# Second feed-forward block of a decoder trunk: the down products of its first two chunks in seven block products

## The chip, the cores and the metric

The kernel runs on one core of a Trainium2 chip. Five engines work beside each other: TensorE (PE, with its weight loads as PEld), VectorE (DVE), ScalarE (ACT), GpSimd (POOL) and SyncE (SP); SP and POOL also issue transfers, each from its own queue. Every engine works through its instructions in order, and waits where an instruction needs the result of another engine or a buffer that is still in use. Matrix products are accumulated in PSUM, in banks of 128 partitions x 512 numbers; everything else lies in SBUF. The metric is the device time of one execution in microseconds.

## The reference, cut to what matters

One step of a trunk with 512 new prompt tokens and 8 sample tokens (520 in all), width 1024, hidden width 2816, all in float32:

```python
h = h + 0.5 * _swiglu(_rms_norm(h, ffn1_norm), w_gate1, w_up1, w_down1)     # FFN1
m, p, c, s = _hybrid_mixer(_rms_norm(h, mix_norm), st_pool, st_conv, st_ssm, ...)
h = h + m
h = h + 0.5 * _swiglu(_rms_norm(h, ffn2_norm), w_gate2, w_up2, w_down2)     # FFN2
return _rms_norm(h, final_norm), new_pool, new_conv, new_ssm

def _swiglu(x, wg, wu, wd):
    return (jax.nn.silu(x @ wg) * (x @ wu)) @ wd

# a sample's new recurrent state (8 samples, 16 heads of 64 x 128):
#   new = exp(dt * A) * old + (dt * x) outer B
```

The new state of each sample is an output that nothing else in the step reads.

## The kernel before, in words

**Numbers in two parts.** Each operand of a large product is cut into a high part and a low part. ScalarE casts the high part, and VectorE subtracts it from the original to get the low part (`split`, L126 and L128; `part`, L228 and L229). Elsewhere a low part is made by a transfer: ScalarE writes minus the high part, and a transfer on POOL's queue adds the original out of memory onto it (`part_by_dma`, L225; L380 and L381 in `load`). `mm3` (L137 to L142) makes a product out of three matmuls of 128 x 128 by 128 x 260: high by high (L138), high by low (L141), low by high (L142). The 520 tokens are two halves of 260.

**Gate and up in seven block products.** The hidden width is 22 tiles of 128. For a tile f the gate and up weights, two halves of the width and two halves of the tokens form products of 2 x 2 blocks, which are made in seven block products for eight. Each is 4 x 3 = 12 matmuls, so a tile is 84. The weights come into a raw pair of buffers (`raw_pair`, two loads of 512 KB). VectorE makes sums of them: s1 of 1024 columns (L409) and s2 in two halves of 512 (L410, L411). These sums are cut into parts shi and slo: "c" from s1, used by products 7 and 5, and "d" from s2, used by 6 and 3. "a" is the first raw half itself, used by products 1 and 2. The last quarter "b" of the raw pair (`quarter`) serves product 4, which is issued in the next tile, right after that tile's product 1. The products accumulate in a bank A and in a double bank BE. ScalarE copies some of them out (L472), VectorE adds them, and `gates`, `silu` and `close` turn them into the gated hidden value.

**FFN1 (`stream`, L527).** Its 22 tiles f go in chunks of 8, 8 and 6. After each of the first two chunks come four Down tiles, `Down(c, d)`: the down product of this chunk for two of the eight output tiles, again in seven block products of 12 matmuls. For this the hidden values are kept in pairs (gq), and `keep_g` (L323) makes seven sums out of each pair of gate values in two parts (gs). The third chunk is done plainly (`down`). In FFN1 the first matmul group of every product is pinned: the products go out in program order.

**FFN2 (`rest`, `step`, `down`, `down_by_half`).** The gate and up products are the same. The down products of its first two chunks are plain: 8 output tiles x 2 halves of the tokens x 8 hidden tiles x 3 = 384 matmuls for a chunk. The third chunk goes by halves of the tokens, so that the final norm can start early. Only two products are pinned; for the rest the order is a planner's, which fills TensorE's queue with whatever is ready by its own estimate. So plain down products and hidden tiles are mixed at the border between them.

**The new states (`new_states`, L1133 on).** There are 16 steps. In each, POOL's queue loads a row `br` (64 KB) and the old state `hs` (256 KB); ScalarE makes `so`, four instructions of 128 x 128 (L1152); VectorE makes hs = hs * sdec + so, four instructions (L1154); POOL's queue stores the result (L1156). `STATES` says how many of these steps go ahead of each output tile of the three plain down products of FFN2. Their buffers, three `br`, three `hs` and two `so`, lie in a pool of their own, st2.

**Homes of weight parts.** Three pairs of whi and wlo (1024 columns each) rotate for the "a" parts and plain down weights (`weight_homes`, L116). `queued` puts an instruction behind a named one on its engine.

Of the kernel before, what the change touches and what calls it, by code (L numbers as in the profile page):

```python
# [17 lines left out]
P = 128  # L18
# [18 lines left out]
NG = 9  # L37
ON_ACT = 4
STATES = ((0, 1, 1, 1, 2, 1, 1, 1), (0, 1, 1, 1, 1, 0, 0, 0), (1, 0, 1, 0, 1, 0, 1, 0))
# [24 lines left out]
def tile_trunk_step(ctx: ExitStack, tc: tile.TileContext, ins: dict, outs: dict):  # L64
# [49 lines left out]
    homes = []  # L114

    def weight_homes(n, name, hp, nb, tags):  # L116
        if hp is wp:
            hp, nb, tags = homes.pop(0) if len(homes) > 1 else homes[0]
        return tuple(hp.tile([P, 1024], F32R, tag=t, bufs=nb, name=f"{t}_{name}")[:, :n] for t in tags)
# [53 lines left out]
    def squares(nx, wx, d, name, home=None):  # L173
        if d == 0:
            nc.scalar.activation(out=nx[2], in_=h[:, d], func=AF.Square)
            return
        sq = home
        if home is None:
            sq = wx.tile([P, 2, HB], F32, tag="tg", bufs=2, name=f"sq_{name}_{d}").rearrange("p b t -> p (b t)")
# [68 lines left out]
    class Ffn:  # L248
# [4 lines left out]
        def __init__(self, nx, i, wx, gp, direct):  # L253
            self.nx, self.i, self.wx, self.gp, self.direct = nx, i, wx, gp, direct
            self.states = None
            self.whole = (2,)
            self.folded = CHUNKS[0] + CHUNKS[1] if i == 1 else 0
            self.held = {} if self.folded else {CHUNKS[0] + 1: None, CHUNKS[0] + CHUNKS[1] + 1: None}
            self.dram, self.gs, self.pairs, self.few, self.later = {}, {}, {}, [], []
# [47 lines left out]
        def gate_home(self, f):  # L307
            if not self.folded:
                return self.wx.tile([P, 2, HB], F32, tag="tg", bufs=2, name=f"tg{self.i}_{f}")
# [13 lines left out]
        def keep_g(self, f, tg):  # L323
            if f >= self.folded:
                if self.folded:
                    if not self.few:
                        self.few = self.cells(f"g{self.i}_{f}")
                    g = self.few.pop().rearrange("p (a b) t -> p a b t", a=2)
                else:
                    g = self.gp.tile([P, 2, 2, HB], F32R, tag="g", bufs=NG, name=f"g{self.i}_{f}")  # L330
                self.g[f] = g
# [16 lines left out]
        def plain_out(self, f):  # L348
# [6 lines left out]
            if f and self.folded:  # L355
# [5 lines left out]
        def load(self, f, first, then, by_dma):  # L361
# [11 lines left out]
            with queued(*first):  # L373
                if self.folded and (f, 0) not in LOW_ON_DVE:
# [14 lines left out]
        def sums(self, f, n, src, raw, d1, by_dma):  # L389
            i, wx = self.i, self.wx  # L390
            s1 = wx.tile([P, 2, 512], F32, tag="sw", bufs=2, name=f"s1_{n}")
            s2 = wx.tile([P, 2, 512], F32, tag="sw", bufs=2, name=f"s2_{n}")
# [4 lines left out]
            else:  # L397
# [3 lines left out]
                s1, s2 = (t.rearrange("p q (j c) -> p q j c", j=4) for t in (s1, s2))  # L401
# [6 lines left out]
            else:  # L408
                nc.vector.tensor_tensor(out=s1, in0=diag, in1=up0, op=ALU.add)  # L409
            nc.vector.tensor_tensor(out=s2[:, 0], in0=s1[:, 1], in1=halves[0][:, 0], op=ALU.add)  # L410
            nc.vector.tensor_tensor(out=s2[:, 1], in0=s2[:, 0], in1=halves[0][:, 1], op=ALU.add)  # L411
            s1, s2 = (t.rearrange("p q c -> p (q c)" if len(t.shape) == 3 else "p q j c -> p (q j c)") for t in (s1, s2))
# [14 lines left out]
        def quarter(self, f, src):  # L427
            n = f"{self.i}_{f}b"
            if self.folded:
                hi, lo = (self.wx.tile([P, 512], F32R, tag=t, name=f"{t}_{n}") for t in ("qhi", "qlo"))  # L430
                h, l = hi, lo
                if len(src.shape) == 3:
                    h, l = (t.rearrange("p (j c) -> p j c", j=4) for t in (hi, lo))
                if isinstance(f, int) and f <= 6 and (f, 1) not in LOW_ON_DVE:
                    home = self.dram[f][1]
                    home = home[:, 512:] if isinstance(f, int) else home.rearrange("p (j q c) -> p q j c", q=2, c=P)[:, 1]
                    part_by_dma(h, l, src, home)
                else:
                    part(h, l, src)
                self.w[f][4] = (hi, lo), range(4)  # L440
                return
            self.w[f][4] = split(src, 512, n, wp, 3, ("whi", "wlo")), range(4)

        def product(self, f, p):
# [7 lines left out]
            if p != 1 and 4 not in self.w[f]:  # L452
                self.quarter(f, self.held[f])
            slot, dst, opens = {1: (0, 0, True), 2: (1, 1, True), 5: (3, 2, True), 6: (5, 0, False),
                                3: (2, 2, False), 7: (4, 0, False), 4: (6, 0, False)}[p]
            opens = opens and (p != 2 or self.i == 2 or f in self.whole)
# [11 lines left out]
            if p == 1 and self.i == 1 and f not in self.whole:  # L468
# [9 lines left out]
        def sum(self, f, home=None):  # L478
            be, a = self.BE[f][:, :, :HB], self.ac[f][0]
            if self.i == 2:  # L480
                nc.vector.tensor_tensor(out=home, in0=be, in1=a, op=ALU.add)
                return home
# [4 lines left out]
        def gates(self, f):  # L487
# [12 lines left out]
            nc.vector.tensor_tensor(out=tg, in0=self.sum(f, tg), in1=self.nx[3].rearrange("p (b t) -> p b t", b=2), op=ALU.mult)  # L500
            if self.i == 2:
                self.silu(f)

        def silu(self, f):
            tg = self.tg[f]
            with queued(*(() if self.i == 2 else (self.copied,))):
# [3 lines left out]
        def close(self, f):  # L510
# [8 lines left out]
            if self.i == 1:  # L519
                self.silu(f)  # L520
# [7 lines left out]
        def stream(self, before, last_chunk):  # L528
# [6 lines left out]
            for t in tiles:  # L535
                self.product(t, 1)
# [7 lines left out]
                if t == 5:  # L544
# [6 lines left out]
            before()  # L551
            self.down(len(CHUNKS) - 1, self.folded, KF, last_chunk)

        def rest(self, before, last_chunk):
            lo = 0
            for c, n in enumerate(CHUNKS):
                hi = lo + n
                last = hi == KF
                for f in range(self.direct if c == 0 else lo + 1, hi if last else hi + 1):
                    self.step(f)  # L560
                if last:
                    self.product(KF - 1, 4)
                    with tc.high_priority():
                        self.close(KF - 1)
                    wd = before()
                else:
                    self.product(hi + 1, 1)
                    self.product(hi, 4)
                    self.close(hi)
                if last and wd is not None:  # L570
                    self.down_by_half(c, lo, last_chunk, wd)
                else:
                    self.down(c, lo, hi, last_chunk if last else None)
                lo = hi

        def step(self, f):
            if f not in self.A:
                self.product(f, 1)
            if f - 1 not in self.g and f > self.direct:
                self.product(f - 1, 4)  # L580
                self.close(f - 1)
            for p in (2, 5, 6, 3, 7) if f in (2, KF - 1) else (5, 6, 3, 7, 2):
# [845 lines left out]
```

## Time and profile before

| | us |
|---|---|
| median of three runs | 975.1 (974.69 to 975.95) |
| the profiled execution | 974.41 |
| its span in the trace | 972.6 |
| TensorE busy | 960.5 (99%) |
| VectorE busy | 825.9 (85%) |
| ScalarE busy | 591.1 (61%) |
| POOL busy | 112.7 (12%) |

The granted clock of TensorE is 0.996 over the span. FFN1 takes about the first third, the mixer the second, FFN2 the last third from about 630 us on. Times of rows are in microseconds unless marked ns. A group of rows is one line of the kernel, an engine, an operation and the tiles that it writes and reads; its mean is the length of one instruction, and neighbours on TensorE overlap. "Idle before" is the time in which the engine stood still ahead of such an instruction, and behind the arrow stands what ended it. The chain is followed back from the last instruction, at each step to what released it.

### The profile page before, as it was taken

The numbers are of one execution on the slowest core, as the hardware profiler recorded it, in microseconds if no ns is written. First come the engines' busy times: TensorE is split into PE (matmuls) and PEld (weight loads), VectorE is DVE, ScalarE is ACT, GpSimd is POOL, SyncE is SP. The second block draws the span as 40 slices with busy tenths as digits, with TensorE's granted clock in tenths as the row PEclk, the third lists the DMA queues.
The fourth block names the chain that finished last, engine by engine and source line by source line (L and its number), as shares of the span: only waits on it lengthen the run. The fifth ranks groups of instructions, "written<-read, shape, count | busy, mean of one in ns | idle before, by whom it ended". The sixth has DMA issues, their size and how long they took to land.

```text
span 972.6 us, 19624 instructions
## 1 busy us (share of the span) xinstructions
PE 960.5 (99%) x7772; PEld 942.4 (97%) x7772; DVE 825.9 (85%) x1374; ACT 591.1 (61%) x1098; POOL 112.7 (12%) x192
## 2 busy tenths in 40 slices
PE   9999999999999999999999999999999999999995
PEld 8999999999999999999999999999999999999995
DVE  6999889899897698789888997999957999667886
ACT  7777666676566455485668655666643666515573
POOL 0111101000010001146331000100013000110010
PEclk9999999999999999999999999999999999999998
DMA  7575644445544233352354324423456333452322
GB/s 213 175 166 144 155 150 115 143 123 147 157 117 131 79 124 110 112 186 88 121 163 126 123 89 122 144 96 110 130 132 201 124 109 113 131 158 88 98 90 89
DMA packets 48444, 126.28 MB, mean 130 GB/s; under 512 B 7064, under 2 KB 15192, under 8 KB 48352
## 3 DMA queue, kind: packets, MB, share of 16 engines
q1 hardware_dynamic: 39840, 104.18, 32.5%
q0 software_dynamic: 8240, 20.71, 10.8%
q8 instruction: 61, 1.00, 0.4%
q14 instruction: 31, 0.25, 0.1%
q10 hardware_dynamic: 272, 0.13, 0.0%
HBM read 117.66 MB, written 7.34 MB: 129 GB/s over the span
## 4 chain that ended last, share of the span: by engine, by line
PE 95%; DVE 3%; ACT 1%; DMA 0%; issue 0%; POOL 0%; DVEq 0%; ACTq 0%
PE A L142 8%; PE A L138 8%; PE A L141 8%; PE BE L141 6%; PE BE L142 6%; PE BE L138 6%; PE dn L142 4%; PE dn L138 4%; PE dn L141 4%; PE P L288 4%; PE wo L138 2%; PE wo L142 2%; PE wo L141 2%; PE inx L138 2%; PE inz L138 2%; PE inz L141 2%
## 5 line engine op out<-in xcount | busy, mean ns | idle before, releaser
L142 PE MATMUL dn<-g,wlo_2d 128*128 128x260 f32 x256 | 72.4, 283 | 0.0
L138 PE MATMUL dn<-g,whi_2d 128*128 128x260 f32 x256 | 72.1, 282 | 0.0
L141 PE MATMUL dn<-g,whi_2d 128*128 128x260 f32 x256 | 72.1, 282 | 0.0
L472 ACT COPY ac<-A 128x260 f32<-128x260 f32 x104 | 38.5, 372 | 31.7 <-PE A L142 31.0
L409 DVE TENSOR_TENSOR s<-raw 128x1024 f32<-128x1024 f32 x39 | 47.5, 1218 | 2.4 <-DMA raw<-in_w2gu 1.5
L138 PEld LDWEIGHTS dn<-g,whi_2d 128*128 128x128 f32 x256 | 48.2, 188 | 0.0
L141 PEld LDWEIGHTS dn<-g,whi_2d 128*128 128x128 f32 x256 | 48.2, 188 | 0.0
L142 PEld LDWEIGHTS dn<-g,wlo_2d 128*128 128x128 f32 x256 | 48.1, 188 | 0.0
L617 DVE SCALAR_TENSOR_TENSOR td<-dn,r_f 128x520 f32<-128x520 f32 (+1 forms) x25 | 16.8, 675 | 34.1 <-PE dn L142 34.1
L126 ACT CAST whi_2d<-raw 128x1024 fp32r<-128x1024 f32 (+1 forms) x18 | 18.5, 1026 | 37.6 <-PE dn L141 15.0
L1156 POOL DMA_DIRECT2D out_nss<-hs x16 | 8.7, 545 | 266.9 <-DVE hs L1154 265.9
L138 PE MATMUL wo<-catg,whi_wo 128*128 128x260 f32 x128 | 37.1, 290 | 0.0
L138 PE MATMUL inz<-xh_mx,whi_inz 128*128 128x260 f32 x128 | 36.6, 286 | 0.0
L138 PE MATMUL inx<-xh_mx,whi_inx 128*128 128x260 f32 x128 | 36.4, 284 | 0.0
L142 PE MATMUL wo<-catg,wlo_wo 128*128 128x260 f32 x128 | 36.3, 283 | 0.0
L141 PE MATMUL inz<-xl_mx,whi_inz 128*128 128x260 f32 x128 | 36.2, 283 | 0.0
L142 PE MATMUL inz<-xh_mx,wlo_inz 128*128 128x260 f32 x128 | 36.2, 283 | 0.0
L141 PE MATMUL inx<-xl_mx,whi_inx 128*128 128x260 f32 x128 | 36.1, 282 | 0.0
L142 PE MATMUL inx<-xh_mx,wlo_inx 128*128 128x260 f32 x128 | 36.1, 282 | 0.0
L141 PE MATMUL wo<-catg,whi_wo 128*128 128x260 f32 x128 | 36.1, 282 | 0.0
L472 ACT COPY ac<-BE 128x260 f32<-128x260 f32 x41 | 15.4, 376 | 26.4 <-PE BE L142 23.9
L1003 DVE SCALAR_TENSOR_TENSOR A<-U,h,A 128x544 f32<-128x544 f32 x36 | 28.9, 802 | 1.1 <-ACT A L1001 0.7
(2147 smaller groups left out, 4376.1 us busy)
## 6 DMA issues: line engine op xcount, KB each, us to landing
raw<-in_w2gu SPq DMA_DIRECT2D x44, 512.0 KB, 3.5
raw<-in_w1gu SPq DMA_DIRECT2D x41, 512.0 KB, 4.2
raw<-in_w_in SPq DMA_DIRECT2D x24, 512.0 KB, 3.5
raw<-in_w1d SPq DMA_DIRECT2D x16, 512.0 KB, 4.7
raw<-in_w2d SPq DMA_DIRECT2D x16, 512.0 KB, 3.6
raw<-in_w_out SPq DMA_DIRECT2D x12, 512.0 KB, 3.6
ab<-scr_acs SPq DMA_DIRECT2D x8, 512.0 KB, 4.9
h<-in_state_ssm SPq DMA_DIRECT2D x16, 256.0 KB, 3.1
```

What stands on the lines that cost most here:

```text
L126: cast = nc.scalar.copy(h, src)
L138: first = nc.tensor.matmul(ps, whi, xhi, start=start, stop=False, **kw)
L141: nc.tensor.matmul(ps, whi, xlo, start=False, stop=False, **kw)
L142: nc.tensor.matmul(ps, wlo, xhi, start=False, stop=stop, **kw)
L288: mm = nc.tensor.matmul(self.banks[f, u][b][:, :HB], ws(self.raw[f][:, u], j + 4 * q), xg[:, slot[q]], start=j == q == 0, stop=j == 3 and ...
L409: nc.vector.tensor_tensor(out=s1, in0=diag, in1=up0, op=ALU.add)
L472: self.copied = nc.scalar.copy(keep, out[:, :HB]).ins
L617: nc.vector.scalar_tensor_tensor(out=o, in0=s, scalar=-0.5, in1=q, op0=ALU.mult, op1=ALU.mult)
L1003: nc.vector.scalar_tensor_tensor(out=A[:, :n], in0=U[:, j : j + n], scalar=w(j), in1=A[:, :n], op0=ALU.mult, op1=ALU.add)
L1156: tc.keep_in_program_order(nc.gpsimd.dma_start(out=outs["nss"][:, b, 4 * g : 4 * g + 4], in_=hs))
```

## The change

FFN2 goes through `stream` as FFN1 does, so that its first two chunks go down as 2 x 4 Down tiles of seven block products. Around this:

- In FFN2 every product from tile 2 on is pinned in program order; silu moves from `gates` to `close`; low parts of "a" are made by transfers on POOL's queue, as in FFN1.
- s1 has one buffer in FFN2 in place of two. s2 has none of its own: it lies in a spare home for f below 4, and later in place in the first raw half. The quarter's two parts share one home, `qs`.
- Two pairs of homes rotate through whi and wlo, and a third pair (thi, tlo) is every third home until the mixer ends. After it, thi is `qs`, and tlo is `room`: two slots for old states.
- A state step writes `so` into a PSUM bank and keeps `hs` in `room`, as long as the pool hg of the last chunk isn't open; the later steps have buffers there. `STATES` now names the Down tiles (one step in each), hidden tiles 17, 19, 20 and 21 (the step at 6 only issues the first loads), and 4 output tiles of the last chunk. The pool st2 is gone.
- `LOW_BY_DMA` names the tiles whose quarter gets its low part by a transfer: 0 to 6, as before in FFN1, and 9, 10 and 11, in both blocks.

```diff
-STATES = ((0, 1, 1, 1, 2, 1, 1, 1), (0, 1, 1, 1, 1, 0, 0, 0), (1, 0, 1, 0, 1, 0, 1, 0))
+STATES = ((1, 1, 1, 1), (6, 17, 19, 20, 21), 4)
+LOW_BY_DMA = (*range(7), 9, 10, 11)
...
-            self.whole = (2,)
-            self.folded = CHUNKS[0] + CHUNKS[1] if i == 1 else 0
+            self.whole = (2,) if i == 1 else (1, 2)
+            self.folded = CHUNKS[0] + CHUNKS[1]
...
-                if self.folded and (f, 0) not in LOW_ON_DVE:
+                if (f, 0) not in LOW_ON_DVE:
...
-            s1 = wx.tile([P, 2, 512], F32, tag="sw", bufs=2, name=f"s1_{n}")
-            s2 = wx.tile([P, 2, 512], F32, tag="sw", bufs=2, name=f"s2_{n}")
+            s1 = wx.tile([P, 2, 512], F32, tag="sw", bufs=3 - i, name=f"s1_{n}")
+            s2 = wx.tile([P, 2, 512], F32, tag="sw", bufs=2, name=f"s2_{n}") if i == 1 else None
+            if i == 2 and isinstance(f, int) and f < 4:
+                s2 = self.qs[1].rearrange("p (q c) -> p q c", q=2)
...
+            s2 = halves[0] if s2 is None else s2
...
-            if f in self.held:
-                self.held[f] = self.gp.tile([P, 512], F32, tag="held", name=f"held{n}")
-                nc.scalar.copy(self.held[f], raw[:, 1, 512:])
+            self.held[f] = halves[1][:, 1]
+            if i == 1:
+                self.quarter(f)
+
+        def quarter(self, f):
+            src = self.held[f]
+            n = f"{self.i}_{f}b"
+            if self.qs is None:
+                hi, lo = (self.wx.tile([P, 512], F32R, tag=t, name=f"{t}_{n}") for t in ("qhi", "qlo"))
             else:
-                self.quarter(f, halves[1][:, 1])
+                hi, lo = self.qs[0][:, :512], self.qs[0][:, 512:]
...
+            if f in LOW_BY_DMA and (f, 1) not in LOW_ON_DVE:
+                part_by_dma(h, l, src, self.dram[f][1][:, 512:])
+            else:
+                part(h, l, src)
...
-                    j == KD // 2 - 1, pin=j == 0 and ((f, p) in ((2, 7), (3, 1)) or self.i == 1), skip_group_check=True)
+                    j == KD // 2 - 1, pin=j == 0 and (self.i == 1 or f != 1), skip_group_check=True)
...
             for t in tiles:
+                for _ in range(STATES[0][t.d] if not isinstance(t, int) else t in STATES[1]):
+                    next(self.states, None)
                 self.product(t, 1)
...
+            wd = before()
+            if wd is None:
+                self.down(len(CHUNKS) - 1, self.folded, KF, last_chunk)
+            else:
+                self.down_by_half(len(CHUNKS) - 1, self.folded, last_chunk, wd)
-
-        def rest(self, before, last_chunk):
...
-        def step(self, f):
...
-        def state_steps(self, c, d):
...
-    f2["ffn"].rest(before2, after2)
+    f2["ffn"].stream(before2, after2)
...
+        spare = [room.rearrange("p (a q n) -> p a q n", a=2, q=4)] * 2
+
         def load(b, g):
-            br = wx.tile([P, P], F32, tag="sb", bufs=3, name=f"br{b}{g}")
+            if "hg" in f2:
+                br = f2["hg"].tile([P, P], F32, tag="br", bufs=3, name=f"br{b}{g}")
+                hs = f2["hg"].tile([P, 4, P], F32, tag="hs", bufs=3, name=f"hs{b}{g}")
+            else:
+                br = tmp.tile([P, HB], F32, tag="ta", name=f"br{b}{g}")[:, :P]
+                hs = spare[g][:, b % 2]
             tc.keep_in_program_order(nc.gpsimd.dma_start(out=br, in_=rows_bc(b, 0, g)))
-            hs = wx.tile([P, 4, P], F32, tag="sh", bufs=3, name=f"hs{b}{g}")
...
-            o = wx.tile([P, 4, P], F32, tag="so", bufs=2, name=f"so{b}{g}")
+            if "hg" in f2:
+                o = f2["hg"].tile([P, 4, P], F32, tag="so", bufs=2, name=f"so{b}{g}")
+            else:
+                o = bank(f"so{b}{g}").rearrange("p (q n) -> p q n", q=4)
```

More of the change, by code (lines that the diff above doesn't have):

```diff
@@ L550, in stream @@
                 self.close(KF - 1)
-            before()
-            self.down(len(CHUNKS) - 1, self.folded, KF, last_chunk)
-        def rest(self, before, last_chunk):
[L555 to L574, printed above, removed]
-        def step(self, f):
[L577 to L582, printed above, removed]
-                self.product(f, p)
-            self.gates(f)
-        def state_steps(self, c, d):
-            for _ in range(STATES[c][d] if self.states is not None else 0):
-                next(self.states)
+            wd = before()
[3 more added lines that the diff above has]
+                self.down_by_half(len(CHUNKS) - 1, self.folded, last_chunk, wd)
         def down(self, c, lo, hi, after):
@@ L753, in before1 @@
         xt1.release()
[L754 removed]
+        w3 = pool("w3", "left")
+        homes[:] = [*homes * 2, (w3, 2, ("whi", "wlo"))]
+        third.append([w3_tile(t, F32R, t) for t in ("thi", "tlo")])
         xa.append(pool("xa", "left"))
```

113 lines of the change are left out of this document (48 added, 65 removed).

## The prediction

> **What bounds the kernel now.** I read the page's busy shares first, then its chain, then the costliest groups, then stretches cut out of the trace.
>
> ```profile
> PE 960.5 (99%) x7772; PEld 942.4 (97%) x7772; DVE 825.9 (85%) x1374; ACT 591.1 (61%) x1098; POOL 112.7 (12%) x192
> PEclk9999999999999999999999999999999999999998
> PE 95%; DVE 3%; ACT 1%; DMA 0%; issue 0%; POOL 0%; DVEq 0%; ACTq 0%
> L142 PE MATMUL dn<-g,wlo_2d 128*128 128x260 f32 x256 | 72.4, 283 | 0.0
> L138 PE MATMUL dn<-g,whi_2d 128*128 128x260 f32 x256 | 72.1, 282 | 0.0
> L141 PE MATMUL dn<-g,whi_2d 128*128 128x260 f32 x256 | 72.1, 282 | 0.0
> L409 DVE TENSOR_TENSOR s<-raw 128x1024 f32<-128x1024 f32 x39 | 47.5, 1218 | 2.4 <-DMA raw<-in_w2gu 1.5
> ```
>
> TensorE is busy 99% at full clock and 95% of the chain is its own: a matmul more or less moves the end. The three groups are the down products of FFN2's first two chunks, 768 matmuls. Their 283 ns is the length of one in a pipeline; what one adds must be read from counts in stretches. Columns below: stretch, its length, busy time and count of each engine, clock, DMA.
>
> ```profile
> core 0: us, PE busy (x) PEld busy (x) DVE busy (x) ACT busy (x) POOL busy (x), PEclk, DMA share, GB/s
> 35.00:314.00 279.00, 278.69 (x2311) 277.63 (x2310) 253.87 (x389) 188.40 (x301) 26.07 (x31) 1.00 0.53 141
> 110.00:151.00 41.00, 40.91 (x341) 40.71 (x340) 36.37 (x58) 23.91 (x38) 3.35 (x4) 1.00 0.54 147
> 637.00:951.00 314.00, 314.00 (x2617) 314.00 (x2616) 256.45 (x407) 170.69 (x305) 22.55 (x42) 1.00 0.40 122
> 703.00:735.00 32.00, 32.00 (x269) 32.00 (x269) 19.70 (x39) 13.63 (x31) 6.62 (x13) 1.00 0.58 149
> 637.00:702.00 65.00, 65.00 (x543) 65.00 (x542) 61.98 (x88) 42.00 (x69) 0.00 (x0) 1.00 0.35 114
> ```
>
> The first stretch is FFN1, whose matmuls are pinned in program order and whose first two chunks already go down in seven block products: 279.00/2311 = 120.7 ns a matmul. The third stretch is FFN2, where only two products are pinned: 314.00/2617 = 120.0 ns and no gap. The fourth, plain down products, gives 32.00/269 = 119.0 ns. VectorE is the second engine: 91% busy in the FFN1 stretch, 95% in FFN2's hidden tiles (fifth), and only 62% in the down stretch, where the new states are stepped now.
>
> **The change part by part.** *Matmuls removed.* Two chunks of 384 become two of 4 Down tiles x 7 products x 12 matmuls = 336. So 96 go; at between 119.0 and 120.7 ns, 11.4 to 11.6 us; I take 11.5, from the middle of the down and tile paces. No other stage loses or gains a matmul.
>
> The Trainium skill, "TensorE: Matmul & The Clock Gate", section "Wait — 56ns, not 53.3ns?", has warm back-to-back matmuls start N / 2.4 GHz plus about 2.5 ns apart. For 260 columns that is an estimate of 110.8 ns, and 96 of them would be worth 10.6 us. This trace never gets there: its best long stretch is at 119.0 ns, and the sum goes by the stretches.
>
> *Order pinned.* FFN2's 19 hidden tiles from tile 3 on and 8 Down tiles, 27 x 84 = 2268 matmuls, now run in program order, as FFN1's do. What FFN1 loses by it is seen in its chain:
>
> ```profile
> 172.23 1.06 ACT shi_12c L126
> 173.29 0.02 issue
> 173.31 0.75 DVE slo_12c L128
> 174.06 0.39 issue
> 174.45 0.15 DVE gq L508
> 174.61 0.19 issue
> 174.79 0.43 DVE gq L522
> 175.22 0.04 issue
> 175.27 0.39 PE A L138
> ```
>
> Where the close of a tile (L508, L522, which frees the bank A) stands behind a low part (slo_12c) on VectorE, the next product into A waits: this piece takes 0.39 where a matmul takes 0.12. By the starts of TensorE's products FFN1 has four of these. In the new order the close stands behind a low part in tiles 2, 6, 10, 12 and 14, five times, so FFN1's pace is the nearest row: 2268 x (120.7 - 120.0) ns = +1.7 us (from 0, if none shows, to twice that). In FFN1 itself the low parts of the quarters of tiles 9 to 11 move from VectorE to accumulating DMAs on POOL; VectorE gets 3 x 0.6 us back and the stall shown above, right behind tile 11, goes: -0.2 (0 to -1.0). Their cover is a full tile of 10 us between need and issue.
>
> *Start of FFN2.* Here VectorE is the bound already:
>
> ```profile
> 632.08 0.69 DVE tg L481
> 633.29 1.22 DVE s L409
> 634.51 0.61 DVE tg L500
> 635.12 1.14 DVE slo_2d L128
> 636.31 0.38 PE A L142
> ```
>
> TensorE is without a ready product three times between 630 and 637, by the starts of its products about 1.0 us in all. The new kernel puts the silu into the close, has one s1 buffer where there were two, and puts the close of tiles 1 and 2 into the pinned order; slo_2d comes some 0.5 us later by the length of one moved instruction. I take +0.5; ends: -1.0 (all three gaps vanish, as gate work leaves VectorE) and +1.8 (the gaps each grow by a 0.6 instruction).
>
> *Vector and scalar work.* Turning pairs of gates into seven sums (L323) and the sums of the Down tiles (L409 to L411) come to FFN2; the plain chunk's td scaling and its low parts go. The cost is that of FFN1's Down tiles: stretch 110 to 151, 36.37/41.00 = 89%, or 8.9 us in a tile of 84 x 119.5 ns = 10.04 us. It is covered as long as VectorE's need stays below 10.04. The low part of d1 goes to POOL's DMA, half of it in a hidden tile and all of it in most Down tiles, which takes 0.6 us (half of L409's 1.2) off VectorE in each hidden tile; that offsets the work on the gate pairs. Sums are costed at nothing under this cover; a tile that went over would cost its excess, one for one.
>
> *States.* They leave the slack of the down stretch (VectorE 62%) and go into 8 Down tiles, 4 late hidden tiles and 4 outputs of the last chunk.
>
> ```profile
> L1154 DVE SCALAR_TENSOR_TENSOR hs<-hs,sdec,so x64: 336/345/351, 711.6 to 941.6; 128x128 f32<-128x128 f32 x64
> L1138 POOL DMA_DIRECT2D hs<-in_state_ssm x16: 537/537/569, 622.3 to 937.8; - x16
>   ACT so L1152: 8.3, 6
> ```
> ```profile
> L1152 ACT ACTIVATE so<-br,sxdt x64: 386/388/407, 700.5 to 940.7; 128x128 f32<-128x128 f32 x64
> ```
>
> The first fence is of the tile hs; its last line says that ACT's `so` waited six times for VectorE's hs, 8.3 us in all. A state is 4 x 345 ns = 1.4 us on VectorE by length; their starts lie 263 ns apart, 1.05 us. A Down tile with a state then needs 8.9 + 1.05 = 9.95 to 8.9 + 1.4 = 10.3 us of VectorE's 10.04. The first 12 states also write `so` into one PSUM bank, so each of ACT's four quarters waits for VectorE's quarter before it. In the instruction order other tile work stands between the quarters on both engines, which hides the hand-over; behind a waiting quarter on VectorE stand the low parts that TensorE needs two to three us later. Bounds: 0, and 12 x (8.3/6 = 1.4) = 16.8 us if each state stalls TensorE as those six stalled ACT. A gain is excluded, since the work was free where it was. I take four stalls of FFN1's size, half of the 8 Down tiles, 4 x 0.25 = +1.0, as 9.95 is nearer the rows' cadence than 10.3.
>
> *Transfers.*
>
> ```profile
> raw<-in_w1d SPq DMA_DIRECT2D x16, 512.0 KB, 4.7
> raw<-in_w2gu SPq DMA_DIRECT2D x44, 512.0 KB, 3.5
> hs<-in_state_ssm POOLq DMA_DIRECT2D x16, 256.0 KB, 4.1
> out_nss<-hs POOLq DMA_DIRECT2D x16, 256.0 KB, 2.3
> br<-scr_bc POOLq DMA_DIRECT2D x16, 64.0 KB, 4.5
> wlo_Down(c=0, d=1)a<-in_w1d POOLq DMA_DIRECT2D x1, 512.0 KB, 5.3
> ```
>
> The quarter's home is now single in FFN2 and read until product 4 of the tile before is done, 24 matmuls (2.9 us) into a tile; its cast and low part take 1.7 more, then raw is free, and its load lands 4.7 later, at 9.3 of 10.04 us. In hidden tiles (3.5) it is 8.1. Covered, with 0.7 us to spare in the Down tiles: 0, up to +0.5 for each of 8 if landing goes to 5.9. On POOL a Down tile queues a br, an hs, a store and one or two accumulates, 4 x 0.54 to 0.85 us of issue; a load of hs waits for the store two states earlier (2.3 us) with the accumulate behind it, which needs 5.3 of the tile's 10: covered. In the tail the last three loads wait for the pool that is freed after the last hidden product; their chain of 4.1 + 1.4 us against 8 us until a bank is needed: 0 (+2 at most).
>
> **Sum.** -11.5 + 1.7 - 0.2 + 0.5 + 1.0 = -8.5 on the profiled execution's 974.41 us (span 972.6 and 1.8 around it): 965.9. That execution lies 0.7 below the median of the runs, 975.1: against the median, 966.6.
>
> **The rivals.** *A, slower: hand-over in the PSUM bank on the path.* If TensorE waits for every hand-over chain, the cost is 1.4 x 12 = 16.8 in place of 1.0: 966.6 + 15.8 = 982.4. The six waits of 1.4 us speak for it, and VectorE's 9.95 of 10.04; against it, the tile work between the quarters and that TensorE reads nothing of a state. Without that term the sum is -9.5, so it decides from 9.5/12 = 0.8 us a state on.
>
> Beside this, the Trainium skill, "PSUM — Partial Sum Buffer", section "PSUM bank collisions raise a hardware error ⚠️", has it that two engines may not be in one bank at the same time and must be kept apart by bank, not by address. By that rule the quarters must alternate although they are disjoint columns; no run here shows a bank shared in this way yet.
>
> *B, VectorE becomes the bound in the Down tiles.* At 10.3 us by length, plus 0.04 to 0.19 us at each of four hand-overs (two of the issue pieces of FFN1's chain), a Down tile takes 10.5 to 11.1: +0.4 to +1.0, eight times, 3.4 to 8.2 in place of 1.0. That gives 969.0 to 973.8, say 971. The 95% of the fifth stretch, with no gap on TensorE, speaks against: there VectorE was as full. For it speaks that now the order is pinned and nothing else can step in.
>
> *C, the change costs nothing.* The pace stays at 120.0, the start's gaps do not grow, the states hide: -11.5 - 0.2, 963.4. For it: the stretch 110 to 151, pinned and with Down tiles, runs at 41.00/341 = 120.2. Against: the four stalls of FFN1 are real.
>
> **How the numbers follow.** My forecast 0.50 (964.5 to 969), B 0.22, C 0.16, A 0.12. A difference under 0.2%, 2 us, is about what a measurement of this kernel can't tell from none. The first three are faster; of A, whose price runs from 0.8 to 1.4 us a state, the quarter nearest 0.8 ends within 2 us: faster 0.88, same 0.03, slower 0.09. The range, 963 to 974, leaves out A and the far ends of C.
>
> **What the changed kernel's profile would show.** Right: 96 fewer matmuls, FFN2 about 8.5 us shorter, TensorE's count by time in its hidden tiles near 120.7 ns with gaps of about 0.25 us where a close stands behind a low part. B: Down tiles longer than 10.04 us and VectorE full in them. A: the chain through `so` and hs, or ACT waiting on VectorE in that pair 12 times or more with TensorE idle behind. C: no gaps at all. Wrong would be the forecast if the chain named a raw load before L409 in FFN2, if the accumulates on POOL came late, or if the start lost over 2 us.

## The result and the profile after

The changed kernel takes 968.29 us (median, 967.53 to 968.55) against 975.1 before: a ratio of 0.9928 with a 95% interval of 0.9911 to 0.9945, so 6.8 us less. A second set of runs beside the experiments gave 968.25 and 0.9929. The prediction was 966.6, in a range of 963 to 974: the sign and the size are right, and 1.7 us of the forecast gain of 8.5 are missing. The profiled execution took 968.40, 6.0 less than that of before.

The page of the changed kernel, busy shares and engines of the chain:

```profile
PE 952.1 (98%) x7676; PEld 931.5 (96%) x7676; DVE 848.9 (88%) x1452; ACT 640.4 (66%) x1191; POOL 147.2 (15%) x231
...
PE 79%; issue 8%; DVE 7%; DMA 2%; ACT 2%; POOL 1%; DVEq 0%; POOLq 0%; ACTq 0%
```

The count has fallen by 96. TensorE still bounds the kernel, but the chain leaves it for a fifth of its length: there are gaps now, and behind each stands another engine. Stretches of the changed kernel, with the columns used before; the second is hidden tiles of FFN2, the last two are its Down tiles.

```profile
core 0: us, PE busy (x) PEld busy (x) DVE busy (x) ACT busy (x) POOL busy (x), PEclk, DMA share, GB/s
35.00:314.00 279.00, 278.11 (x2305) 276.90 (x2304) 251.46 (x386) 189.60 (x303) 28.67 (x34) 1.00 0.53 143
...
643.00:702.00 59.00, 58.53 (x486) 58.12 (x485) 52.55 (x83) 42.42 (x69) 10.78 (x14) 1.00 0.64 158
703.00:743.00 40.00, 39.66 (x327) 39.28 (x326) 38.42 (x68) 28.59 (x55) 8.45 (x13) 1.00 0.71 184
826.00:867.00 41.00, 40.38 (x333) 39.97 (x332) 38.24 (x68) 28.69 (x55) 8.42 (x13) 1.00 0.69 179
```

In the Down tiles VectorE is 96 and 93% busy (38.42 of 40.00 us, 38.24 of 41.00), and TensorE is no longer busy all the time. The gaps in FFN2, read off the starts of TensorE's matmuls, fall into three kinds.

The first stands ahead of hidden tiles 4, 8, 12, 14 and 16, where the close of tile 2, 6, 10, 12 and 14 has to free the bank A. The chain ahead of tile 8:

```profile
688.59 1.06 ACT shi_8c L134
689.65 0.03 issue
689.68 1.23 DVE slo_8c L136
690.90 0.34 DVE gq L507
691.24 0.35 DVE gq L520
691.59 0.04 issue
691.63 0.39 PE A L146
```

The close (L507, L520) sits right behind the low part slo_8c. With the slow first matmul behind it, the gap ahead of tile 4 costs 0.67 us and each of the other four some 0.33: 2.0 in all.

The second kind is in the Down tiles: 0.8 at 703 to 705, 0.3 at 828 and 0.9 at 859. Beside these, 0.6 in tile 18 stands behind the low part slo_18d, which is late on VectorE. The end of the chain at 705:

```profile
703.23 0.25 ACT so L1131
703.48 0.05 issue
703.53 0.62 ACT gs L236
704.15 0.95 ACT whi_Down(c=0, d=1)a L380
705.10 0.28 ACT BE_Down(c=0, d=0)_8669 L476
705.38 0.04 issue
705.43 0.39 PE BE_Down(c=0, d=0)_8669 L146
```

The copy that TensorE needs (L476) comes behind a state's `so`, the parts of gate values and the next tile's cast. But `so` takes 0.3 us of this queue, and what makes the queue late lies ahead of it, on VectorE. There the sum of the first Down tile (L412) stands waiting for its raw weights, and everything behind it moves: the close of tile 7, the gate parts, the copy. VectorE in the changed kernel, in a second trace of the same kernel, and in a kernel that has the states' transfers but neither `so` nor `hs` (both are described below):

```profile
693.58 1.23 DVE L412 TENSOR_TENSOR s_Down(c=0, d=0)_8656<-raw 128x1024 f32<-128x1024 f32 x1 [2.00 <-DMA raw<-in_w2d]
```
```profile
692.27 1.23 DVE L412 TENSOR_TENSOR s_Down(c=0, d=0)_8656<-raw 128x1024 f32<-128x1024 f32 x1 [0.64 <-DMA raw<-in_w2d]
```
```profile
694.19 1.23 DVE L412 TENSOR_TENSOR s_Down(c=0, d=0)_8648<-raw 128x1024 f32<-128x1024 f32 x1 [2.10 <-DMA raw<-in_w2d]
```

In the second trace the sum and the copy both come 1.3 us earlier, with the same `so` between them, and there is no gap. In the third the gap is 0.8, without any `so`. The gap at 828 goes the same way: it is there when the sum waits 1.4 and 2.2 us (first and third), and not when it waits 0.7 (second). So these two gaps hang on a raw load that lands late.

The third kind is a transfer too, the accumulated low part of a quarter that lands late. The chain in tile 10, where product 4 of tile 9 needs it:

```profile
747.71 7.56 DMA qs<-in_w2gu
755.27 0.04 issue
755.31 0.39 PE A L150
```

### The profile page after: what moved, and what is told of

Its sections match the earlier page's. It is cut to its first block, busy times and chain, and to the rows that moved or that the text cites. A ratio compares the mean times of both kernels' runs of the same rounds, so it can differ in the third digit from the quotient of the medians.

```text
span 966.6 us, 19705 instructions
## 1 busy us (share of the span) xinstructions
PE 952.1 (98%) x7676; PEld 931.5 (96%) x7676; DVE 848.9 (88%) x1452; ACT 640.4 (66%) x1191; POOL 147.2 (15%) x231
## 4 chain that ended last, share of the span: by engine, by line
PE 79%; issue 8%; DVE 7%; DMA 2%; ACT 2%; POOL 1%; DVEq 0%; POOLq 0%; ACTq 0%
PE A L146 6%; PE A L150 6%; PE A L149 6%; PE BE L149 5%; PE BE L146 4%; PE BE L150 4%; PE P L295 4%; PE wo L146 2%; PE wo L150 2%; PE wo L149 2%; PE inx L146 2%; PE inz L146 2%; PE inz L149 2%; PE inz L150 2%; PE inx L149 2%
## 5 line engine op out<-in xcount | busy, mean ns | idle before, releaser
L476 ACT COPY ac<-A 128x260 f32<-128x260 f32 x85 | 31.5, 371 | 33.0 <-PE A L150 30.9
L412 DVE TENSOR_TENSOR s<-raw 128x1024 f32<-128x1024 f32 x39 | 47.5, 1217 | 3.6 <-DMA raw<-in_w2gu 2.2
L476 ACT COPY ac<-BE 128x260 f32<-128x260 f32 x41 | 15.4, 376 | 27.8 <-PE BE L150 25.8
L295 PE MATMUL P<-x,raw 128*128 128x260 f32 x128 | 29.2, 390 | 0.0
L295 PEld LDWEIGHTS P<-x,raw 128*128 128x128 f32 x128 | 24.9, 196 | 3.9
L1131 ACT ACTIVATE so<-br,sxdt 128x128 f32<-128x128 f32 x64 | 22.6, 375 | 7.4 <-DVE room L1133 4.0
L1089 ACT ACTIVATE junk<-h 128x128 f32<-128x128 f32 x64 | 19.8, 309 | 10.1 <-DVE h L1086 8.7
L506 ACT ACTIVATE gq<-gq 128x520 f32<-128x520 f32 x37 | 23.6, 639 | 3.3 <-DVE gq L501 3.0
L501 DVE TENSOR_TENSOR gq<-BE,r_f 128x520 f32<-128x520 f32 x37 | 25.6, 691 | 0.1
L150 PE MATMUL A<-xth_f,qs 128*128 128x260 f32 x84 | 23.8, 283 | 0.2 <-DMA qs<-in_w2gu 0.2
L146 PE MATMUL A<-xth_f,qs 128*128 128x260 f32 x84 | 23.9, 285 | 0.0
L237 DVE TENSOR_TENSOR gs<-gq,gs 128x780 fp32r<-128x780 f32 (+1 forms) x28 | 23.2, 829 | 0.8 <-ACT gs L236 0.8
L1232 DVE TENSOR_TENSOR h<-wo,h 128x260 f32<-128x260 f32 x48 | 19.0, 417 | 5.6 <-PE wo L150 5.6
L149 PE MATMUL A<-xtl_f,qs 128*128 128x260 f32 x84 | 23.7, 282 | 0.0
L485 DVE TENSOR_TENSOR BE<-BE,ac 128x260 f32<-128x260 f32 (+1 forms) x41 | 18.4, 448 | 5.5 <-PE BE L150 5.5
```

The source lines that it names most:

```text
L146: first = nc.tensor.matmul(ps, whi, xhi, start=start, stop=False, **kw)
L149: nc.tensor.matmul(ps, whi, xlo, start=False, stop=False, **kw)
L150: nc.tensor.matmul(ps, wlo, xhi, start=False, stop=stop, **kw)
L237: low = nc.vector.tensor_tensor(out=lo, in0=s, in1=hi.bitcast(F32), op=ALU.subtract)
L295: mm = nc.tensor.matmul(self.banks[f, u][b][:, :HB], ws(self.raw[f][:, u], j + 4 * q), xg[:, slot[q]], start=j == q == 0, stop=j == 3 and ...
L476: self.copied = nc.scalar.copy(keep, out[:, :HB]).ins
```

## The experiments

**The 96 matmuls alone.** The kernel before, with nothing but these left out:

```diff
+                m = n - 1 if self.i == 2 else n
                 for b in range(2):
-                    for k in ks:
+                    for k in ks[:m]:
...
-                        mm3(banks[d][b], ..., k == 0, k == n - 1)
+                        mm3(banks[d][b], ..., k == 0, k == m - 1)
```

> The kernel before, with the last of the eight hidden tiles left out of the plain down products of FFN2's first two chunks and of the third: per chunk of eight 48 matmuls fewer, so 96 there, while every other instruction stays; the third chunk goes by halves and keeps all. The output lacks those terms. By the stretches 96 x 119.5 ns = 11.5: 963.6. By 110.8 ns a matmul 10.6: 964.5. If down products were partly a cover for other work, less: 965 to 968.

964.42 against 975.37 of before beside it, a ratio of 0.9890 (0.9877 to 0.9904): 11.0 us less, with 9.4 to 12.0 as bounds. The matmuls were on the path, and next to no cover: in its trace FFN2 has two gaps that the kernel before hasn't, 0.7 and 0.5, both behind late work of VectorE. The interval holds the 11.5 of the stretches. It also holds 10.6, the estimate from the Trainium skill's "TensorE: Matmul & The Clock Gate" (section "Wait — 56ns, not 53.3ns?"), and so doesn't tell one from the other. The trace leans to the stretches: from tile 3 to the last down product FFN2 is 10.4 shorter with 1.3 of new gaps in it, so 11.7, or 121 ns for each of the 96.

**No pinned order in FFN2.**

```diff
-pin=j == 0 and (self.i == 1 or f != 1)
+pin=j == 0 and (self.i == 1 or (f, p) in ((2, 7), (3, 1)))
```

> The changed kernel with FFN2's products pinned only where the kernel before pinned them (two products). Theory: the planner, free to put other matmuls in front of a product whose bank isn't free, takes back the five A gaps of FFN2, 2.0 us: 966.0 to 966.6. Rival: gaps stay or move, since in an order fixed ahead nothing steps in either: 967.8 to 969.

986.83, a ratio of 1.0120 (1.0106 to 1.0134) to the kernel before: 18.6 us above the changed kernel. Neither number was near. Its waits on TensorE:

```profile
engine line waited for: us in total, times, longest us
PE A L146 <- ACT ac L476: 8.4, 14, 1.8
PE A L150 <- DMA qs<-in_w2gu: 1.7, 1, 1.7
```

A planner's free order is fixed before the run as well. Here it puts product 4 of a tile right behind the product into A whose copy it must wait for, where program order has product 1 of the next tile between the two. That happens fourteen times in hidden tiles (8.4 us), and in seven Down tiles for 3.3 more. The pinned order isn't only a price of 1.7 us: with this planner, Down tiles in FFN2 don't pay without it.

**The close ahead of the low part.** In both blocks slo_c is queued behind the close of the tile two before.

```diff
-            nc.vector.tensor_tensor(out=tg[:, 0], in0=self.A[f][:, :HB], ...)
+            self.shut = nc.vector.tensor_tensor(out=tg[:, 0], in0=self.A[f][:, :HB], ...).ins
...
-                e1 = split(s1, 1024, f"{n}c", wx, 2, ("shi", "slo"))
+                e1 = split(s1, 1024, f"{n}c", wx, 2, ("shi", "slo"), (self.shut,) if self.shut else ())
```

> The low part slo of a tile is put behind the close of the tile two before it, in both feed-forward blocks. Theory (the close behind a low part is what stalls A): the five gaps in FFN2 (0.67 and four of 0.33) and the three left in FFN1 ahead of tiles 12, 14, 16 (0.3 each) go: 2.0 to 2.9 us less, 965.4 to 966.3. Rival: the low part is then late itself and TensorE waits there, in product 5: 968.3 within 0.5, or above.

975.76, the whole gain lost. Where the two only changed places, ahead of tile 14 in both blocks and of tile 12 in FFN2, the gap is gone, as the theory says (ahead of tile 12 in FFN1 the changed kernel had none to lose, against what was written). Ahead of tile 8 it grew to 1.6 and ahead of tile 16, in both blocks, to 2.2: the constraint let the next tile's sums (L480, L485) in front of the close too, and ahead of tile 8 they wait 1.8 us for copies of ScalarE. Another 1.6 went to a late quarter in tile 12 of FFN2, and 1.5 to a halved clock of TensorE behind the gap ahead of tile 16 in FFN1 (shown with the next kernel). So the cause of the gaps stands, but this edit isn't its cure.

**The quarters' low parts back on VectorE.**

```diff
-LOW_BY_DMA = (*range(7), 9, 10, 11)
+LOW_BY_DMA = (*range(7),)
```

> The changed kernel with the low parts of the quarters of tiles 9, 10 and 11 back on VectorE in both blocks. Theory: the accumulating transfer for tile 10 lands 7.6 us after its issue and TensorE waits for it, 0.6 at 167 and 0.5 at 755; without it these go, and the gap ahead of tile 12 in FFN1 comes back (0.3): 967.3 to 967.8. Rival: VectorE, with 0.6 more in three tiles, is late elsewhere by as much: 968.3 within 0.4.

975.56, a ratio of 1.0001 (0.9992 to 1.0010): with this one line undone nothing of the gain is left. The late quarter in tile 10 is gone, but ahead of tile 12 of FFN2 TensorE now stands still for 5.1 us. VectorE's instructions there (start, length, instruction, and what it waited for):

```profile
772.61 1.23 DVE L136 TENSOR_TENSOR slo_12c<-s,shi_12c 128x1024 fp32r<-128x1024 f32 x1 [0.16 <-ACT shi_12c L134]
773.75 0.69 DVE L501 TENSOR_TENSOR gq<-BE,r_f 128x520 f32<-128x520 f32 x1
774.36 0.42 DVE L480 TENSOR_TENSOR ac<-ac 128x260 f32<-128x260 f32 x1
774.70 0.43 DVE L485 TENSOR_TENSOR BE<-BE,ac 128x260 f32<-128x260 f32 x1
775.03 1.21 DVE L136 TENSOR_TENSOR slo_12d<-raw,shi_12d 128x1024 fp32r<-128x1024 f32 x1
776.17 1.21 DVE L412 TENSOR_TENSOR s<-raw 128x1024 f32<-128x1024 f32 x1
777.30 0.68 DVE L384 TENSOR_TENSOR wlo_13a<-raw,whi_13a 128x512 fp32r<-128x512 f32 x1
777.90 0.69 DVE L501 TENSOR_TENSOR gq<-BE,r_f 128x520 f32<-128x520 f32 x1
778.51 0.42 DVE L507 TENSOR_TENSOR gq<-ac,gq 128x260 f32<-128x260 f32 x1
778.85 0.42 DVE L520 TENSOR_TENSOR gq<-A,gq 128x260 f32<-128x260 f32 x1
```

From slo_12c on there is no pause in it. The gate product of tile 10 (the first L501) has slipped behind slo_12c, its silu then behind a cast on ScalarE, and the close of tile 10 (L507, L520) behind six more instructions; TensorE waits 4.8 us for it. When it goes on, its clock is halved for some 3.4 us (PEclk, third number from the end):

```profile
779.75:783.09 3.34, 3.34 (x18) 3.34 (x17) 0.81 (x2) 0.36 (x1) 0.00 (x0) 0.50 0.36 64
```

Its matmuls start 0.22 apart there in place of 0.12, which costs another 1.5 us. Is the late close a matter of the place in the queue, or of too much work? The same kernel with the order mended at this one place:

```diff
+            if self.i == 2 and f == 10:
+                self.gated[f + 2] = gated.ins
...
+            if self.i == 2 and f == 10:
+                self.shut[f + 2] = shut.ins
...
-                e1 = split(s1, 1024, f"{n}c", wx, 2, ("shi", "slo"))
-            e2 = split(s2, 1024, f"{n}d", wx, 2, ("shi", "slo"))
+                e1 = split(s1, 1024, f"{n}c", wx, 2, ("shi", "slo"), (self.gated[f],) if f in self.gated else ())
+            with queued(*((self.shut[f],) if f in self.shut else ())):
+                e2 = split(s2, 1024, f"{n}d", wx, 2, ("shi", "slo"))
```

(`gated` is the gate product in `gates`, `shut` the last product of `close`.)

> The kernel quarters_on_dve (975.6), whose trace has TensorE idle 5.1 us ahead of tile 12 of FFN2 because VectorE's gate product of tile 10 stood behind slo_12c, so silu came behind whi_13a on ScalarE and the close of tile 10 behind slo_12d, the sum s of tile 13 and wlo_13a. Here the same work, with slo_12c put behind that gate product and both parts 12d behind the close. Theory (the place in the queue costs, not the amount of work): the gap falls from 5.1 to 1.5 to 2.5 (silu still stands behind shi_12d), and the time to 972 to 973. Rival (VectorE has too much to do in tiles 9 to 12): the gap stays over 4, 975 or more.

970.40, a ratio of 0.9954 (0.9941 to 0.9968): 5.2 of the 7.3 us are back (4.6 of 7.0 by the two ratios to the kernel before). VectorE's instructions at the place now (their lines have moved by two or three: L502 is the gate product, L510 and L523 are the close):

```profile
770.52 0.69 DVE L502 TENSOR_TENSOR gq<-BE,r_f 128x520 f32<-128x520 f32 x1
771.13 1.22 DVE L136 TENSOR_TENSOR slo_12c<-s,shi_12c 128x1024 fp32r<-128x1024 f32 x1
772.26 0.42 DVE L481 TENSOR_TENSOR ac<-ac 128x260 f32<-128x260 f32 x1
772.69 0.44 DVE L486 TENSOR_TENSOR BE<-BE,ac 128x260 f32<-128x260 f32 x1
773.13 0.43 DVE L510 TENSOR_TENSOR gq<-ac,gq 128x260 f32<-128x260 f32 x1
773.47 0.42 DVE L523 TENSOR_TENSOR gq<-A,gq 128x260 f32<-128x260 f32 x1
```

The gap is 1.6, as expected, and the time lower than expected: behind the shorter gap the clock stays at 1.00, so 3.5 us of gap and 1.5 of slow matmuls are gone together. The work is the same, so most of the 5.1 was order.

**What the states cost.** Without any state step (the new sample states aren't computed):

```diff
-    f2["ffn"].states = f2["states"](f2["ffn"].qs[1])
+    f2["ffn"].states = iter([None] * 17)
```

> All 16 state steps of FFN2 are left out (loads, ScalarE's so, VectorE's hs, stores); the new sample states aren't computed. Theory: the steps cause the stalls of TensorE in the Down tiles (0.8 us at 703 to 705, 0.3 at 828, 0.9 at 859 in the changed kernel's trace) and the late low part in tile 18 (0.6 at 881): 2.0 to 2.6 us less than the changed kernel's 968.3, so 965.7 to 966.3, and no product into BE of a Down tile waits for ScalarE. Rival: those stalls are the Down tiles' own (the turning of gate pairs at the chunk's end): 968.3 within 0.5.

964.59, 3.7 less than the changed kernel, a little more than expected. The gaps at 705, 828 and 859 and in tile 18 are gone, and from tile 21 to the end it is 1.0 shorter: together 3.6. One new gap came, 0.8 in the Down tiles, behind a late accumulate, which leaves 2.8. The two profiled executions differ by 2.6 (this one was the slowest of its four, 1.2 above their median), so the gaps account for what the traces can show. Without the states' transfers the sum of the first Down tile no longer waits in either chunk.

`so` without a hand-over for each quarter, ScalarE's four first:

```diff
             for q in range(4):
                 j = 4 * g + q
                 ... nc.scalar.activation(out=o[:, q], ...)
+            for q in range(4):
+                j = 4 * g + q
                 ... nc.vector.scalar_tensor_tensor(out=hs[:, q], ...)
```

> Per state, ScalarE's four so go ahead of VectorE's four hs in program order, so that the bank is handed over once and not four times. If the hand-over is what costs: the Down stalls shrink by half or more, 967.0 to 967.6, and ScalarE's waits on VectorE at so fall from many to a few. If only the amount of work counts: 968.3 within 0.5.

969.88, slower by 1.6 than the changed kernel. Of `so`, what ended ScalarE's idle time (us, times), in the changed kernel and then in this one:

```profile
  DVE room L1133: 4.0, 9
```
```profile
  DVE room L1135: 0.2, 1
```

The hand-over is all but gone, and so are the gaps of the Down tiles. But the raw loads came earlier as well: the sums whose waits go with the three gaps wait 1.0, 0.8 and 0.0 us here, in place of 2.0, 1.4 and 2.2, so this run doesn't tell the one cause from the other. New gaps came in tiles 9, 10, 17 and 19 (0.6, 0.7, 1.6 and 0.4), the largest at a late slo_17d, and at a late quarter in tile 11 (0.8). The expectation for the Down tiles held, that for the time did not.

Next, ScalarE's part left out, VectorE's kept (it adds the row `br` itself, so the states lack their scale):

```diff
-                    nc.scalar.activation(out=o[:, q], in_=br, func=AF.Copy, scale=...)
...
-                                                   in1=o[:, q], op0=ALU.mult, op1=ALU.add))
+                                                   in1=br, op0=ALU.mult, op1=ALU.add))
```

> The changed kernel without ScalarE's so: VectorE adds the row br itself in place of so, so the new states are wrong by their scale; VectorE's 64 instructions, all transfers and their places stay. Theory 1 (the hand-over through the PSUM bank, and ScalarE's queue behind it, make the states' 3.7 us): at least half of it goes, 964.6 to 966.4, and no product into BE of a Down tile waits for a copy. Theory 2 (VectorE's share makes it): 967.5 to 968.5, and tile 18's gap stays. In both the tail stays.

970.36: again not faster. The stretches of its Down tiles, ahead of them those of the kernel without states:

```profile
703.00:743.00 40.00, 40.00 (x335) 40.00 (x334) 35.00 (x54) 24.06 (x38) 3.44 (x4) 1.00 0.56 145
826.00:867.00 41.00, 40.45 (x336) 40.24 (x335) 35.16 (x55) 24.34 (x38) 3.44 (x4) 1.00 0.55 141
```
```profile
703.00:743.00 40.00, 40.00 (x334) 40.00 (x333) 38.84 (x70) 23.85 (x38) 9.03 (x14) 1.00 0.73 196
826.00:867.00 41.00, 41.00 (x342) 41.00 (x342) 38.68 (x70) 24.35 (x38) 10.14 (x16) 1.00 0.75 186
```

With VectorE as full as in the changed kernel (38.8 and 38.7 us), TensorE is busy throughout. So the Down gaps are not VectorE's fullness. They aren't shown to be the hand-over either, as theory 1 has it, for here too the raw loads came earlier (the same three waits are 1.2, 0.9 and 0.2). The gap at 859 is there in the five traces in which the sum of that chunk's last Down tile waits 2.0 to 2.5 us and states are stepped. It isn't there with that wait and no states, nor with the states handed over as in the changed kernel and a wait under 0.5 (the two kernels with fewer steps in the tail, below). It takes both, and which part each has stays open.

The time is lost in one gap of 3.8 in tile 17 and in 1.5 of halved clock behind it: a sum stands waiting 1.4 us for its raw weights, and all four instructions of a state have moved between it and slo_17d.

Transfers alone (states loaded and stored, not stepped):

```diff
-            for q in range(4):
-                j = 4 * g + q
-                ... nc.scalar.activation(out=o[:, q], ...)
-                ... nc.vector.scalar_tensor_tensor(out=hs[:, q], ...)
```

> The states are loaded and stored but not stepped: so and hs instructions are left out, all transfers stay. If the work and its hand-over between ScalarE and VectorE make the stalls: as without any states, 965.7 to 966.3. If the transfers do (0.58 MB more in each Down tile): 968.3 within 0.5, and the raw and low-part loads land as late as in the changed kernel.

975.12, spread over 971 to 980, slower than with the work in it. Without the steps a store can follow its load at once: POOL issues them 0.5 us apart, and a raw load issued beside them takes 9.04 us to land. VectorE in this kernel:

```profile
717.81 1.23 DVE L412 TENSOR_TENSOR s_Down(c=0, d=2)_8899<-raw 128x1024 f32<-128x1024 f32 x1 [5.01 <-DMA raw<-in_w2d]
718.96 1.22 DVE L136 TENSOR_TENSOR slo_Down(c=0, d=1)d<-raw,shi_Down(c=0, d=1)d 128x1024 fp32r<-128x1024 f32 x1
```

VectorE stands 5.0 us at the sum of the next tile, and behind it waits the low part that TensorE needs: a gap of 2.5, and one of 2.2 in the second chunk with 1.5 of halved clock behind it. Neither of the two expectations fits; it shows instead what a raw load 4 us late costs. The gaps at the first Down tile of each chunk are here too (0.8 and 0.5), as shown at the start, though nothing of a state is computed.

**Fewer steps in the tail.**

```diff
-STATES = ((1, 1, 1, 1), (6, 17, 19, 20, 21), 4)
+STATES = ((1, 1, 1, 1), (6, 16, 17, 19, 20, 21), 3)
```

and, in the second kernel,

```diff
+STATES = ((1, 1, 1, 1), (6, 16, 17, 18, 19, 20, 21), 2)
```

> One state step is moved from the last chunk's outputs (four there, now three) ahead of hidden tile 16; all other steps are one place earlier. Without any states the stretch from tile 21 to the end is 1.0 us shorter. Theory (state work on VectorE late in the tail delays the last sums): a quarter to all of this 1.0 goes, 967.3 to 968.0. Rival: tile 16 and the tiles behind it, at 9.9 of 10.04 us of VectorE with it, lose as much: 968.3 to 969.

> As three_in_tail, with one more step moved, ahead of hidden tile 18. Theory: the tail is 0.5 to 1.0 shorter, 967.3 to 967.8. Rival: tile 18, where the low part slo_18d is late by 0.6 already, loses 1 us or more by VectorE's further 1.05: 969 or more.

968.64 and 969.30. In both, the stretch from tile 21 to the end is 1.1 to 1.2 us shorter than in the changed kernel, the whole of what the tail had to give, and the changed kernel's gaps in the Down tiles and in tile 18 are gone. Others stand in their place: at the late slo_17d (1.3 and 2.0) and in the Down tiles (0.9 and 0.6; 1.2 and 0.8). No version that computes everything beat the changed kernel.

**The changed kernel again.**

> The changed kernel beside these, for the same chip and the same runs of the kernel before: 968.3 within 0.5. Gaps of A where a close stands behind a low part should be at the same places and of the same size; those that hang on a transfer's landing (quarters of tiles 4 and 10) may differ by some tenths.

968.25. In its trace the five gaps of A are at the same places and of the same size. What hangs on transfers isn't: the quarters of tile 4 in FFN1 and of tile 9 in FFN2 were in time, those of tiles 9 and 10 in FFN1 late by 0.2 each, and the Down tiles have two gaps, 0.3 at 735 and 0.8 at 858, which make 1.0 in place of 2.0. Its profiled execution is 1.5 shorter: FFN2 by 1.5 and FFN1 by 0.6, it began 0.3 earlier, and between the two blocks it took 0.9 longer.

## Why the prediction was right, and where it was off

*Matmuls removed, -11.5:* right. Alone they gave -11.0, with an interval that holds the forecast, and -11.7 in the trace without the gaps that came.

*Order pinned, +1.7:* right as a sum. The five gaps stand at the five forecast tiles and make 2.0. What the forecast didn't say is that the planner's order is far dearer, by 18.6.

*FFN1, -0.2:* wrong. The gap behind tile 11 went, as forecast (0.3), but the quarters' accumulates were costed at nothing under "a full tile of 10 us between need and issue", and they hadn't 10 us. The home is read until product 4 of the tile before, and the same product needs it a tile later: that of tile 10 was issued at 159.8 and needed at 167.0, and it landed after 7.6 us, 0.6 of loss. The kernel before had five such transfers, which landed after 5.8 to 7.0 us; these rows weren't used. From tile 2 to the first product of the third chunk FFN1 took 0.75 more than before in the first trace and 0.2 more in the second. Of the 0.75, 0.6 belongs to the quarter of tile 4, which goes by transfer in both kernels, so it isn't shown to come from the change. And `LOW_BY_DMA` was costed for FFN1 alone. In FFN2, where it decides the place of the close of tile 10, it carries 7.3 us, of which the order mended at one place gave back 5.2. This is the weakest step, though it doesn't show in the sum; that the change had this line, for a forecast of 0.2 us, was luck.

*Start of FFN2, +0.5:* wrong sign, inside its bounds. The three gaps became one. With the slow matmuls behind them, as the other gaps are counted, they were 0.3, 0.5 and 0.5, and the one is 0.7: -0.6.

*States, +1.0:* mis-sized; 3.7 by leaving them out. In the first trace that is 2.0 in the Down tiles, 0.6 in tile 18 and 1.0 in the tail, where nothing was forecast. Of the 2.0, 1.1 hangs on late raw loads and not on the stalls that were forecast, and in the second trace the Down tiles lose only 1.0. Against before, 0.2 to 0.4 of the tail is new, read from the last down product and from the last uses of slo_21c and slo_21d to the end: there the kernel before had state work too.

*Transfers, 0:* too low. The late quarter of tile 9 in FFN2 cost 0.5 in one trace, none in the other. The 0.7 us to spare in the Down tiles were spent: the 512 KB loads of FFN2's down weights took 4.7 and 5.3 us in the median of the two traces, 3.6 before. What ended VectorE's idle time ahead of the sums (L412) in the second trace, us and times:

```profile
  DMA raw<-in_w2d: 4.9, 4
...
  DMA raw<-in_w1d: 2.2, 4
```

Four of FFN2's eight Down tiles wait for their raw weights, 1.2 us each, more than twice as long as FFN1's. In the two traces of the changed kernel TensorE has a gap behind each such wait of 1.4 us or more, and behind none under 1.0.

By these terms the first profiled execution comes to -11.5 + 2.0 + 0.75 - 0.6 + 2.6 + 0.3 + 0.5, and -0.2 as its first product started earlier: -6.15 of the measured -6.0. The second comes to -11.5 + 2.0 + 0.2 - 0.6 + 1.7 + 0.3, with -0.5 for the earlier start and +0.9 between the blocks: -7.5, as measured. That the sum came out within 2 us is in part luck: the start was better than forecast by 1.1, which hides almost a third of what the order, FFN1, the states and the transfers cost beyond the forecast in the first trace (3.65).

*The rivals.* A is out: the hand-over exists (nine waits, 4.0 us on ScalarE), but all gaps of the Down tiles together cost TensorE 2.0 and 1.0 us, not 16.8. The Trainium skill's rule that two engines don't share a bank ("PSUM — Partial Sum Buffer", section "PSUM bank collisions raise a hardware error ⚠️") fits the alternation, which ended when each engine's four went in a row. B was right in that the Down tiles lose: by the stretches one takes 84 x 40.00/327 = 10.3 us, over the 10.04 that was named as its sign. It was too dear (2.0 where its range began at 3.4), and wrong in its mechanism: VectorE at 97% alone made no gap there. C is out by the gaps. What the prediction named last as what would make it wrong, a raw load before the sum and accumulates that come late, is in the changed kernel itself, 1.1 and 0.5 us in the first trace, and did the damage in two of the experiments.

## What to carry to other kernels

On engines that work in order, a change that fills the second engine to 95% can make the order of its queue worth more than its amount of work. Here one line that took 0.6 us from it in three tiles held 7 us, of which 5 came back by putting three instructions in their places. Price such a line by where the instructions land in the new order, not by their length. A cure that adds one constraint to a planned order must be read in the whole order it yields, since here each of them moved something else. And when a gap stands at the end of a long queue, follow the queue back to the first wait that differs between two traces: the `so` that stood in this queue was not what made it late.

## What the runs showed of the hardware that was not expected

In five of the traces TensorE's granted clock fell to 0.50 for about 3.4 us shortly after a gap of 2.0 to 5.1 us, once in each, and this cost 1.3 to 1.6 us beside the gap. Behind three other gaps of 2.1 to 2.5 us the clock stayed at 1.00, and no shorter gap was followed by such a fall. What decides it these runs don't show.

The landing time of an accumulating transfer of 256 KB on POOL's queue varies between 3.5 and 7.9 us within the changed kernel, and from run to run at the same place: the quarter of tile 4 in FFN1 landed after 7.7 us in one trace and held TensorE up, and after 6.8 us in the other and did not. Raw loads of 512 KB, 3.5 us in the median before, took up to 9.0 where stores of states followed their loads at once.
